# A two-layer hybrid trunk on one Trainium2 core: the residual kept token-major, with down and output projections that move 512 weight columns past stationary activations

## The chip, the cores and the metric

One core of a Trainium2 chip runs one program. The metric is the device time of one execution in microseconds (us), lower is better; each execution is one launch. Engines are named as the profile names them: PE is the matrix engine (PEld its weight loads), DVE, ACT and POOL work on elements, SP issues most transfers (SPq is its queue).

## The reference, cut to what matters

The input x is 256 tokens by 2048 features in fp32. Two layers follow, each with a mixer and a feed-forward part, all added to the residual x:

```python
for layer in range(2):
    h = rmsnorm(x, norm_w[layer, 0])
    x = x + (even_mixer(h, ...) if layer == 0 else odd_mixer(h, ...))
    h = rmsnorm(x, norm_w[layer, 1])
    x = x + swiglu(h, ffn_w_gu[layer], ffn_w_down[layer])
return rmsnorm(x, final_norm_w)
```

`even_mixer` is a projection, a causal convolution with layer norm, sparse attention and an output projection of 2048 by 2048. `odd_mixer` is a projection to 8192 columns, a gated recurrence in chunks and an output projection of 2048 by 2048. `swiglu` projects to two times 5632 columns and down to 2048. Five norms run over the 2048 features: two per layer and the final one.

## The kernel before, in words

**Layout.** Features lie on the partitions: the residual is 16 tiles `x[f]` of 128 features by 256 tokens. The normed activations lie so too, in 16 tiles `xhl(k)` (input of a stage) or `mhl(k)` (input of a down or output projection), each in two parts: a high part rounded to the engine's fp32r type and the low part that is left. A norm puts only its weight into the tile; the factor per token is applied when a product leaves PSUM (`self.bc`, one row of factors on all partitions).

**Weights.** `units` (lines 187 to 213) loads 1 MB of weights at a time into one of three `raw` buffers (SP queue), and ACT writes the high part `whi` and DVE (in part POOL) the low part `wlo`, 1024 columns of a partition at a time; three buffers of each. Each product is hi times hi, hi times lo and lo times hi.

**Two kinds of product.** `w_job` (215 to 247) makes 256 output features: each 128 by 128 block of weights is stationary and the activations of 256 tokens move past it. Its usual form has two matmuls for a block: the high weights past both parts of the activations (512 columns, line 240) and the low weights past the high part (256 columns, line 241; lines 237 and 238 for the last block), so a PSUM tile holds two halves that must be added. Its joint form has three matmuls of 256 columns (lines 233 to 235) and one sum. `x_job` (249 to 267) makes 512 output features for 128 tokens at a time: the activations are stationary, 512 weight columns move, three matmuls (lines 260 to 262) for each block of 128 features and each half `tb` of the tokens. Before the change only the odd mixer's `i` and `g` columns and the even mixer's values use it.

**Where the change lies.** The down projections of both layers (in `ffn`, three slabs of 16, 14 and 14 blocks of the hidden features, each with 8 chunks of 256 columns) and the odd output projection are `w_job`; the very last chunk of a layer and the even output projection are its joint form. Each finished tile `f` goes through `add_residual` (ACT copy, line 309, DVE add, 310, POOL add, 311; in the joint form one DVE add, 306) and, in the last slab or the mixer's last pass, `norm_tile`: ACT squares it, POOL adds the squares up (323), and `split` writes the parts of the next stage's `xhl` (ACT 139, DVE 140). `norm_done` calls `inv_rms`: matmuls with ones sum the squares over the partitions (160), DVE takes the root (146 to 151), and a matmul with a diagonal makes `self.bc` (177, 181). The final norm multiplies x by `bc` (1306) and stores it in four transfers.

**Order.** A scheduler orders instructions by a simulated timeline and by priorities (the work on finished tiles is raised by 600); each engine then runs its own list strictly in that order. Between `in_order()` and `traced = None` PE's order is instead the program's: the attention part of the even mixer with its first two output passes (input blocks 0 to 7 and 8 to 11), and the odd mixer up to the end of the first chunk of its output projection. The third even pass (blocks 12 to 15) and all of `ffn` are free. `drive` puts a list of background steps between the units of a list of jobs.

Of the kernel before, what the change touches and what calls it, by code (L numbers as in the profile page):

```python
# [10 lines left out]
F32 = mybir.dt.float32  # L11
# [21 lines left out]
COLS_B = (  # L33
    ("fnw", 16),
    ("convb", 8),
# [33 lines left out]
class Net:  # L69
# [82 lines left out]

    def inv_rms(self, sums, n, copy=True):


        nc = self.nc
        ps = self.mx()
        for tb in range(2):
            for i, q in enumerate(sums):
                nc.tensor.matmul(  # L160
                    ps[:, tb : tb + 1],
                    q[:, tb * 128 : tb * 128 + 128],
                    self.ones[:, 0:1],
                    start=(i == 0),
                    stop=(i == len(sums) - 1),
                )
        v = self.tile(self.tp, [128, 2], "rs_v", bufs=2)
        nc.vector.tensor_scalar(v, ps[:, 0:2], 1.0 / n, EPS, op0=ALU.mult, op1=ALU.add)
        tok = self.tile(self.tp, [128, 2], "rs_tok", bufs=2)
        self.rsqrt(tok, v, "rs")  # L170
        diag = self.t256("rs_diag", bufs=1)
        for tb in range(2):
            nc.vector.tensor_scalar(
                diag[:, tb * 128 : tb * 128 + 128], self.ca("ident"), tok[:, tb : tb + 1], None, op0=ALU.mult
            )
        pb = self.mx()
        nc.tensor.matmul(pb[:, :S], self.ones, diag, start=True, stop=True)
        if not copy:
            return tok, pb[:, :S]
        bc = self.t256("rs_bc", bufs=2)  # L180
        nc.scalar.copy(bc, pb[:, :S])
        return tok, bc
# [65 lines left out]

    def x_job(self, w, nkt, ncols, src, evac):

        nc = self.nc
        ps = [self.tile(self.ps_acc, [128, 512], "acc") for _ in range(2)]
        for k0, nu, hi, lo in self.units(w, nkt, ncols):
            last = k0 + nu == nkt
            for tb in range(2):
                t = slice(tb * 128, tb * 128 + 128)
                for i in range(nu):
                    k = k0 + i
                    o = ps[tb][:, :ncols]
                    nc.tensor.matmul(o, src(k)[:, 0, t], hi[:, i, :], start=(k == 0), stop=False)  # L260
                    nc.tensor.matmul(o, src(k)[:, 0, t], lo[:, i, :], start=False, stop=False)  # L261
                    nc.tensor.matmul(o, src(k)[:, 1, t], hi[:, i, :], start=False, stop=(k == nkt - 1))  # L262
                if last:
                    with self.tc.high_priority(offset=600):
                        evac(tb, ps[tb])
            yield

# [33 lines left out]

    def add_residual(self, f, ps, joint=False):
        nc = self.nc
        x = self.x[f]
        if joint:
            nc.vector.tensor_add(x, ps[:, :S], x)
            return
        c = self.t256("e_c")
        nc.scalar.copy(c, ps[:, S:])
        nc.vector.tensor_add(x, ps[:, :S], x)  # L310
        nc.gpsimd.tensor_add(x, x, c)  # L311

    def norm_tile(self, f, w, xhl):

        nc = self.nc
        x = self.x[f]
        if f == 0:
            self.ssq = self.t256("n_ssq", bufs=2)
            nc.scalar.activation(self.ssq, x, AF.Square)
        else:  # L320
            sq = self.t256("n_sq", bufs=2)
            nc.scalar.activation(sq, x, AF.Square)
            nc.gpsimd.tensor_add(self.ssq, self.ssq, sq)
        if xhl is not None:
            self.split(xhl(f), x, w[:, f : f + 1])

# [15 lines left out]
    def norm_done(self):  # L342
        self.tok, self.bc = self.inv_rms([self.ssq], D)

# [4 lines left out]

    def ffn(self, wgu, wdn, xhl, final_tile):  # L350
        nc = self.nc
        chunk = 0
        for s, (h0, nh) in enumerate(SLABS):
# [25 lines left out]
            jobs = []  # L379
            for c in range(8):  # L380

                def evac_d(nt, ps, c=c):
                    f = 2 * c + nt
                    self.add_residual(f, ps, joint=last and c == 7)
                    if last:
                        final_tile(f)

                jobs.append((-(-nh // 4), self.w_job(wdn[s][c], nh, mhl, evac_d, joint=last and c == 7)))
            self.drive(jobs)
# [3 lines left out]
    def even(self, xhl, start):  # L393
# [60 lines left out]
        def ln_steps():  # L454
# [24 lines left out]
            def root():  # L479
                self.rsqrt(st["r"], st["v"], "n_s")  # L480

# [65 lines left out]
        def evac_c(kv):  # L547
# [31 lines left out]
            [job(14 + i, evac_q(1, i)) for i in range(2)] + [job(10, evac_c(0)), job(11, evac_c(1))],  # L579
            ln_rest + [turn_gates, self.lower_bound],  # L580
            until=0.8,
# [16 lines left out]
        def evac_res(c, xhl2=None):  # L598
            def f(nt, ps):
                self.add_residual(2 * c + nt, ps, joint=True)  # L600
                if xhl2 is not None:
                    self.norm_tile(2 * c + nt, self.nw(1), xhl2)

            return f

        def out_jobs(k0, k1, xhl2=None):
            n = (k1 - k0 + 3) // 4 * 2
            src = lambda k: self.mhl(k0 + k)
            return [
                (n, self.w_job(wo[c, :, k0:k1], k1 - k0, src, evac_res(c, xhl2), joint=True)) for c in range(8)  # L610
            ]
# [372 lines left out]
    def odd(self, xhl):  # L984
# [245 lines left out]
        xhl2 = self.new_xhl()  # L1230

        def evac_res(c):
            def f(nt, ps):
                self.add_residual(2 * c + nt, ps)
                self.norm_tile(2 * c + nt, self.nw(3), xhl2)

            return f

        wo = a["od_out"]
        js = [(4, self.w_job(wo[c], KD, mhl, evac_res(c))) for c in range(8)]  # L1240
        self.drive(js[:1], O[3][1], until=0.75)
        self.traced = None
# [6 lines left out]
    def run(self):  # L1249
        nc, a = self.nc, self.a  # L1250
        self.cst_a = self.tile(self.fix, [128, NA], "cst_a")
        self.cst_b = self.tile(self.fix, [128, NB], "cst_b")
        nc.sync.dma_start(self.cst_a, a["cst_a"])
        xq = [self.tile(self.fix, [128, 4, S], f"x{i}") for i in range(4)]
        self.x = [xq[f // 4][:, f % 4, :] for f in range(KD)]
        self.ones = self.tile(self.fix, [128, 128], "ones")
        nc.vector.memset(self.ones, 1.0)
        self.mean1024 = self.tile(self.fix, [128, 128], "mean1024")
        nc.vector.memset(self.mean1024, 1.0 / 1024)

        xhl = self.new_xhl()
        sq = []

        def first_norm(i):

            x = xq[i]
            nc.sync.dma_start(x, a["x"][:, i * 4 : i * 4 + 4, :])
            w = self.nw(0)[:, i * 4 : i * 4 + 4].unsqueeze(2).to_broadcast([128, 4, S])
            xw = self.quarter(f"mhl{i}", (128, 2, 4, S), F32)
            nc.vector.tensor_mul(xw[:, 0], x, w)  # L1270
            xhl(4 * i)
            q = xhl.have[i]
            nc.scalar.activation(q[:, :, 0, :], xw[:, 0], AF.Copy)
            nc.vector.tensor_sub(q[:, :, 1, :], xw[:, 0], q[:, :, 0, :].bitcast(F32))  # L1274
            sq.append(xw[:, 1])
            with self.tc.high_priority(offset=-60):
                nc.scalar.activation(sq[i], x, AF.Square)
                if i:
                    nc.gpsimd.tensor_add(sq[0], sq[0], sq[i])

        def first_sums():
            first_norm(3)
            t = sq[0]
            nc.gpsimd.tensor_add(t[:, 0:2], t[:, 0:2], t[:, 2:4])
            nc.gpsimd.tensor_add(t[:, 0], t[:, 0], t[:, 1])
            self.ssq = t[:, 0]
            self.norm_done()

        first_norm(0)
        xhl = self.even(xhl, [lambda: first_norm(1), lambda: first_norm(2), first_sums])  # L1290

        nxt = self.new_xhl()
        self.ffn(a["gu0"], a["dn0"], xhl, lambda f: self.norm_tile(f, self.nw(2), nxt))
        xhl = self.odd(nxt)

        def last(f):
            self.norm_tile(f, None, None)
            x = self.x[f]
            nc.scalar.activation(x, x, AF.Copy, scale=self.cb("fnw")[:, f : f + 1])

        self.ffn(a["gu1"], a["dn1"], xhl, last)
        self.norm_done()
        bc = self.bc.unsqueeze(1)
        for i in (3, 0, 1, 2):
            eng = nc.gpsimd if i == 3 else nc.vector
            eng.tensor_mul(xq[i], xq[i], bc.to_broadcast([128, 4, S]))
            nc.sync.dma_start(a["out"][:, 4 * i : 4 * i + 4, :], xq[i])

# [108 lines left out]
```

## Time and profile before

| | |
|---|---|
| median of 3 runs | 2411.53 us (2409.87 to 2411.82) |
| the profiled execution's own time | 2411.09 us |
| its span in the trace | 2409.3 us |
| PE, share of the span | 98% |
| DVE, ACT, POOL | 64%, 49%, 26% |
| mean busy share of the 16 DMA engines | about 54% |

In the trace times run from the span's start. A row of a group gives line, engine, operation, output and inputs with shapes, count, busy time and the mean length of one. Matmuls are pipelined: the length of one is longer than the distance to the next, so PE's pace is read from starts and from whole stretches, not from lengths.

### The profile page before, as it was taken

How to read it: one execution, taken by the hardware profiler on the slowest of the kernel's cores; microseconds unless marked ns; L12 is line 12 of the kernel's file. 1: busy time of each engine (PE TensorE's matmuls, PEld its weight loads, DVE VectorE, ACT ScalarE, POOL GpSimd, SP SyncE). 2: the span in 40 equal slices, each digit the busy share in tenths (PEclk: the TensorE clock that was granted, in tenths of full speed). 3: DMA queues.
4: the chain of work that ended last, by engine and by line, in shares of the span. 5: the costliest groups of instructions: out<-in, count | busy, mean ns of one | idle time of the engine just before them, and what ended most of it. 6: DMA issues, size and time to landing. Idle time of an engine off the chain costs nothing.

```text
span 2409.3 us, 36579 instructions
## 1 busy us (share of the span) xinstructions
PE 2364.6 (98%) x14492; PEld 2086.6 (87%) x14492; DVE 1540.8 (64%) x2335; ACT 1173.1 (49%) x1729; POOL 625.2 (26%) x608
## 2 busy tenths in 40 slices
PE   6999999999999999999999999999999999999997
PEld 6999889888888888888888888888888888888886
DVE  7996578565555555657657777766555555555555
ACT  4435456554444544545544444455544445445454
POOL 5754524111111121114213333332111111121123
PEclk9999999999999999999999999999999999999998
DMA  6554524555555556555555445455555555565553
GB/s 208 176 174 154 179 78 151 193 188 183 189 192 189 180 183 200 188 180 186 195 178 175 159 156 175 140 185 185 190 192 183 186 191 192 175 194 191 192 175 123
DMA packets 62269, 427.88 MB, mean 178 GB/s; under 512 B 6928, under 2 KB 7056, under 8 KB 15248
## 3 DMA queue, kind: packets, MB, share of 16 engines
q1 hardware_dynamic: 61776, 425.01, 53.7%
q8 instruction: 113, 1.85, 0.3%
q10 hardware_dynamic: 320, 0.52, 0.1%
q14 instruction: 60, 0.49, 0.1%
HBM read 422.89 MB, written 2.10 MB: 176 GB/s over the span
## 4 chain that ended last, share of the span: by engine, by line
PE 94%; DVE 3%; issue 1%; POOL 1%; ACT 0%; DMA 0%; DVEq 0%; SPq 0%; POOLq 0%; ACTq 0%
PE acc L240 44%; PE acc L241 23%; PE acc L233 4%; PE acc L235 3%; PE acc L234 3%; PE acc L238 3%; PE acc L260 3%; PE acc L262 3%; PE acc L261 3%; PE acc L237 2%; PE mx L1089 1%; DVE wlo L208 1%; PE mx L677 1%; PE mx L855 0%; PE mx L782 0%
## 5 line engine op out<-in xcount | busy, mean ns | idle before, releaser
L208 DVE TENSOR_TENSOR wlo<-raw,whi 128x1024 fp32r<-128x1024 f32 (+1 forms) x749 | 959.0, 1281 | 659.7 <-ACT whi L207 648.3
L207 ACT ACTIVATE whi<-raw 128x1024 fp32r<-128x1024 f32 (+1 forms) x809 | 843.5, 1043 | 889.5 <-PE acc L240 596.7
L240 PE MATMUL acc<-xhl,whi 128*128 128x512 f32 x3120 | 1089.5, 395 | 0.0
L241 PE MATMUL acc<-xhl,wlo 128*128 128x256 f32 x3120 | 843.8, 280 | 0.0
L240 PEld LDWEIGHTS acc<-xhl,whi 128*128 128x128 f32 x3120 | 573.0, 188 | 113.0 <-issue 0.8
L241 PEld LDWEIGHTS acc<-xhl,wlo 128*128 128x128 f32 x3120 | 589.0, 189 | 25.1
L240 PE MATMUL acc<-mhl,whi 128*128 128x512 f32 x1500 | 520.1, 395 | 0.0
L241 PE MATMUL acc<-mhl,wlo 128*128 128x256 f32 x1500 | 398.7, 280 | 0.0
L297 POOL TENSOR_TENSOR e_u<-e_s,rs_bc 128x256 f32<-128x256 f32 x192 | 149.8, 781 | 937.7 <-DVE e_s L290 901.0
L240 PEld LDWEIGHTS acc<-mhl,whi 128*128 128x128 f32 x1500 | 273.9, 188 | 50.9
L241 PEld LDWEIGHTS acc<-mhl,wlo 128*128 128x128 f32 x1500 | 283.3, 189 | 15.4
L311 POOL TENSOR_TENSOR x<-x,e_c 128x256 f32<-128x256 f32 x108 | 109.1, 1023 | 422.0 <-DVE x L310 422.0
L208 POOL TENSOR_TENSOR wlo<-raw,whi 128x1024 fp32r<-128x1024 f32 (+1 forms) x60 | 145.2, 2421 | 141.3 <-ACT whi L207 130.4
L233 PE MATMUL acc<-xhl,whi 128*128 128x256 f32 (+1 forms) x528 | 149.8, 289 | 9.5 <-ACT whi L207 9.5
L235 PE MATMUL acc<-xhl,wlo 128*128 128x256 f32 (+1 forms) x528 | 150.2, 290 | 6.3 <-DVE wlo L208 4.0
L288 ACT COPY e_c<-acc 128x256 f32<-128x256 f32 x208 | 77.6, 373 | 157.9 <-PE acc L238 157.9
L234 PE MATMUL acc<-xhl,whi 128*128 128x256 f32 (+1 forms) x528 | 150.4, 288 | 1.4 <-DVE xhl L1274 1.4
L290 DVE TENSOR_TENSOR e_s<-acc,e_c 128x256 f32<-128x256 f32 x208 | 87.4, 422 | 67.6 <-ACT e_c L288 65.3
L261 PE MATMUL acc<-wlo,xhl 128*128 128x512 f32 x288 | 112.5, 391 | 0.0
L262 PE MATMUL acc<-whi,xhl 128*128 128x512 f32 x288 | 112.2, 390 | 0.0
L233 PEld LDWEIGHTS acc<-xhl,whi 128*128 128x128 f32 (+1 forms) x528 | 102.5, 195 | 9.7 <-ACT whi L207 9.5
L260 PE MATMUL acc<-whi,xhl 128*128 128x512 f32 x288 | 110.3, 395 | 0.0
(228 smaller groups left out, 2518.9 us busy)
## 6 DMA issues: line engine op xcount, KB each, us to landing
raw<-in_gu SPq DMA_DIRECT2D x176, 1024.0 KB, 5.0
raw<-in_dn SPq DMA_DIRECT2D x64, 1024.0 KB, 5.1
raw<-in_od_fq SPq DMA_DIRECT2D x32, 1024.0 KB, 5.0
raw<-in_od_ig SPq DMA_DIRECT2D x32, 1024.0 KB, 4.9
raw<-in_ev_in SPq DMA_DIRECT2D x30, 1024.0 KB, 5.0
raw<-in_dn SPq DMA_DIRECT2D x32, 768.0 KB, 4.4
raw<-in_od_out SPq DMA_DIRECT2D x16, 1024.0 KB, 5.0
raw<-in_ev_out SPq DMA_DIRECT2D x8, 1024.0 KB, 5.1
```

The source lines that it names most:

```text
L207: nc.scalar.activation(hi[:, :m], rs, AF.Copy)
L208: eng.tensor_sub(lo[:, :m], rs, hi[:, :m].bitcast(F32))
L233: nc.tensor.matmul(o[:, :S], h, a[:, 0, :], start=first, stop=False)
L234: nc.tensor.matmul(o[:, :S], h, a[:, 1, :], start=False, stop=False)
L235: nc.tensor.matmul(o[:, :S], l, a[:, 0, :], start=False, stop=end)
L240: nc.tensor.matmul(o, h, both, start=first, stop=False)
L241: nc.tensor.matmul(o[:, S:], l, a[:, 0, :], start=False, stop=False)
L260: nc.tensor.matmul(o, src(k)[:, 0, t], hi[:, i, :], start=(k == 0), stop=False)
L261: nc.tensor.matmul(o, src(k)[:, 0, t], lo[:, i, :], start=False, stop=False)
L262: nc.tensor.matmul(o, src(k)[:, 1, t], hi[:, i, :], start=False, stop=(k == nkt - 1))
L297: self.nc.gpsimd.tensor_mul(u, s, self.bc)
L311: nc.gpsimd.tensor_add(x, x, c)
```

## The change

The residual becomes one tile of tokens by features: partition t holds tokens t and 128 + t with all 2048 features. Down and output projections use `x_job` with 512 columns, four chunks in place of eight; `add_residual` is one DVE add of 128 by 512 from PSUM. For the three norms that feed a stage, `square` takes the sum of squares per token on ACT, and `turn_norm` turns each chunk's 8 blocks of 128 by 128 on PE into PSUM, from where `split` reads them. The sums lie per token, so the ones matmuls of these norms go. The first norm still reads a feature-major x, into scratch; the token-major copy is a second 2 MB load inside the even mixer. The final norm's weight is a 1 MB tile, spread over the partitions; x is stored in eight transfers.

```diff
-    def inv_rms(self, sums, n, copy=True):
+    def inv_rms(self, sums, n):
...
-        for tb in range(2):
-            for i, q in enumerate(sums):
-                nc.tensor.matmul(
-                    ps[:, tb : tb + 1],
-                    q[:, tb * 128 : tb * 128 + 128],
-                    self.ones[:, 0:1],
...
-        nc.vector.tensor_scalar(v, ps[:, 0:2], 1.0 / n, EPS, op0=ALU.mult, op1=ALU.add)
+        nc.vector.tensor_scalar(v, sums, 1.0 / n, EPS, op0=ALU.mult, op1=ALU.add)
...
-    def x_job(self, w, nkt, ncols, src, evac):
+    def x_job(self, w, nkt, ncols, src, evac, fine=False):
...
+                if fine and tb == 0:
+                    yield
...
+    def add_residual(self, c, tb, ps):
+        x = self.x[:, tb, c * 512 : c * 512 + 512]
+        self.nc.vector.tensor_add(x, ps, x)
+
+    def square(self, c, tb):
+        if c == 0 and tb == 0:
+            self.ss = self.tile(self.tp, [128, 2, 4], "n_ss", bufs=2)
+        sq = self.tile(self.tp, [128, 512], "n_sq", bufs=1)
+        self.nc.scalar.activation(
+            sq, self.x[:, tb, c * 512 : c * 512 + 512], AF.Square, accum_out=self.ss[:, tb, c : c + 1]
+        )
+
+    def turn_norm(self, c, w, xhl):
...
+        for f2 in range(4 * c, 4 * c + 4, 2):
+            pt = self.mx()
+            for i in range(4):
+                f, tb = f2 + i // 2, i % 2
+                x = self.x[:, tb, f * 128 : f * 128 + 128]
+                nc.tensor.transpose(pt[:, i * 128 : i * 128 + 128], x, self.ca("ident"))
+            for i in range(2):
+                f = f2 + i
+                self.split(xhl(f), pt[:, i * 256 : i * 256 + 256], w[:, f : f + 1])
+
+    def to_norm(self, w, xhl):
+        def f(c, tb):
+            self.square(c, tb)
+            if tb == 1:
+                self.turn_norm(c, w, xhl)
+        return f
...
     def norm_done(self):
-        self.tok, self.bc = self.inv_rms([self.ssq], D)
+        s = self.tile(self.tp, [128, 2], "n_s", bufs=2)
+        self.nc.vector.tensor_reduce(out=s, in_=self.ss, op=ALU.add, axis=AX.X)
+        self.tok, self.bc = self.inv_rms(s, D)
...
-                jobs.append((-(-nh // 4), self.w_job(wdn[s][c], nh, mhl, evac_d, joint=last and c == 7)))
+                jobs.append((nh // 2, self.x_job(wdn[s][c], nh, 512, mhl, evac_d)))
...
-            ln_rest + [turn_gates, self.lower_bound],
+            [lambda: nc.sync.dma_start(self.x, a["xt"])] + ln_rest + [turn_gates, self.lower_bound],
...
-                (n, self.w_job(wo[c, :, k0:k1], k1 - k0, src, evac_res(c, xhl2), joint=True)) for c in range(8)
+                (k1 - k0, self.x_job(wo[c, :, k0:k1], k1 - k0, 512, src, evac_res(c, xhl2), fine=True))
+                for c in range(4)
...
-        js = [(4, self.w_job(wo[c], KD, mhl, evac_res(c))) for c in range(8)]
-        self.drive(js[:1], O[3][1], until=0.75)
+        js = [(8, self.x_job(wo[c], KD, 512, mhl, evac_res(c))) for c in range(4)]
+        self.drive(js[:1], O[3][1], until=0.5)
...
+        def last(c, tb):
+            self.square(c, tb)
+            x = self.x[:, tb, c * 512 : c * 512 + 512]
+            eng = nc.vector if c == 3 else nc.gpsimd
+            eng.tensor_mul(x, x, fnw[:, c * 512 : c * 512 + 512])
+
+        nc.sync.dma_start(fnw, a["fnw"])
         self.ffn(a["gu1"], a["dn1"], xhl, last)
...
+        for c in range(4):
+            for tb in range(2):
+                x, r = self.x[:, tb, c * 512 : c * 512 + 512], tok[:, tb : tb + 1]
+                if (2 * c + tb) % 3 == 1:
+                    nc.scalar.activation(x, x, AF.Copy, scale=r)
+                else:
+                    nc.vector.tensor_scalar(x, x, r, None, op0=ALU.mult)
+                nc.sync.dma_start(a["out"][:, tb, c * 512 : c * 512 + 512], x)
```

The weights of these projections are laid out on the host in chunks of 512 columns in place of 256.

## Rows read from the trace of the kernel before

**Rows 1.** The page: busy time by engine, PE's granted clock in 40 slices, the chain.

```profile
PE 2364.6 (98%) x14492; PEld 2086.6 (87%) x14492; DVE 1540.8 (64%) x2335; ACT 1173.1 (49%) x1729; POOL 625.2 (26%) x608
...
PEclk9999999999999999999999999999999999999998
...
PE 94%; DVE 3%; issue 1%; POOL 1%; ACT 0%; DMA 0%; DVEq 0%; SPq 0%; POOLq 0%; ACTq 0%
```

**Rows 2.** Stretches: length, then busy us (instructions) by engine, granted clock, DMA share, GB/s.

```profile
594.79:684.39 89.60, 89.60 (x514) 78.40 (x513) 47.93 (x52) 39.74 (x50) 11.92 (x17) 1.00 0.58 188
841.19:919.86 78.67, 78.67 (x449) 68.65 (x448) 43.90 (x51) 35.47 (x50) 18.52 (x16) 1.00 0.58 191
1076.71:1155.62 78.91, 78.91 (x478) 70.11 (x477) 58.24 (x66) 46.04 (x78) 31.20 (x29) 1.00 0.58 191
1201.36:1244.90 43.54, 43.54 (x194) 36.04 (x192) 22.82 (x21) 19.97 (x21) 4.78 (x4) 1.00 0.58 194
1560.33:1651.00 90.67, 90.67 (x524) 79.34 (x523) 62.61 (x81) 49.66 (x79) 29.18 (x29) 1.00 0.54 177
2313.08:2391.99 78.91, 78.91 (x477) 70.09 (x475) 42.83 (x50) 44.91 (x76) 30.63 (x29) 1.00 0.46 150
248.85:395.00 146.15, 139.73 (x1176) 125.13 (x1175) 98.98 (x331) 76.15 (x199) 51.80 (x62) 0.98 0.36 119
395.00:414.02 19.02, 19.02 (x161) 19.02 (x160) 18.84 (x30) 16.31 (x33) 12.62 (x12) 1.00 0.70 232
```

**Rows 3.** PE's timeline in the third even output pass: start, length, line, instruction.

```profile
413.54 0.28 PE L235 MATMUL acc<-mhl,wlo 128*128 128x256 f32 x1
...
413.90 0.28 PE L235 MATMUL acc<-mhl,wlo 128*128 128x256 f32 x1
```

**Rows 4.** The chain in the odd mixer, at one of its transposes (start, us on the chain).

```profile
1345.24 0.87 PE mx L1212 x8
```

**Rows 5.** The group of these transposes: count, then busy us and mean ns of one.

```profile
L1212 PE MATMUL mx<-cst_a,K 128*128 128x128 f32 x32 | 4.3, 272 | 0.0
```

**Rows 6.** The timeline after the even mixer's last tile (in brackets: idle before, releaser).

```profile
420.66 0.61 PE L160 MATMUL mx<-ones,n_ssq 128*128 128x1 f32 x4 [0.45 <-POOL n_ssq L323]
420.81 1.21 DVE L208 TENSOR_TENSOR wlo<-raw,whi 128x1024 fp32r<-128x1024 f32 x1
```

**Rows 7.** Groups of DVE, ACT and POOL on tiles like those of the change.

```profile
L1186 DVE COPY K<-mx 128x512 f32<-128x512 f32 x8 | 5.5, 687 | 4.4 <-PE mx L1180 4.4
...
L140 DVE SCALAR_TENSOR_TENSOR mhl<-mx,cst_b,mhl 128x256 fp32r<-128x256 f32 x16 | 7.0, 478 | 0.4 <-ACT mhl L139 0.2
...
L1188 ACT ACTIVATE o_sq<-mx 128x512 f32<-128x512 f32 x8 | 4.8, 597 | 7.3 <-DVE K L1186 7.3
...
L311 POOL TENSOR_TENSOR x<-x,e_c 128x256 f32<-128x256 f32 x108 | 109.1, 1023 | 422.0 <-DVE x L310 422.0
```

**Rows 8.** Transfers: count, KB each, median us from issue to landing.

```profile
raw<-in_ev_out SPq DMA_DIRECT2D x8, 1024.0 KB, 5.1
raw<-in_ev_out SPq DMA_DIRECT2D x16, 512.0 KB, 3.6
...
out<-x SPq DMA_DIRECT2D x4, 512.0 KB, 3.3
```

**Rows 9.** The timeline of the end, from PE's last projection matmul on.

```profile
2391.87 0.28 PE L235 MATMUL acc<-mhl,wlo 128*128 128x256 f32 x1
...
2392.18 0.42 DVE L306 TENSOR_TENSOR x<-acc,x 128x256 f32<-128x256 f32 x1 [0.29 <-PE acc L235]
...
2394.81 0.16 DVE L168 TENSOR_SCALAR rs_v<-mx 128x2 f32<-128x2 f32 x1 [2.20 <-PE mx L160]
...
2396.97 0.48 DVE L173 TENSOR_SCALAR rs_diag<-cst_a,rs_tok 128x128 f32<-128x128 f32 x2
...
2399.17 5.64 DVE L1306 TENSOR_TENSOR x<-x,rs_bc 128x1024 f32<-128x1024 f32 x3 [1.72 <-ACT rs_bc L181]
...
2400.42 4.75 SPq L1307 DMA_DIRECT2D out<-x  x4
```

More of the change, by code (lines that the diff above doesn't have):

```diff
@@ L33 @@
 COLS_B = (
-    ("fnw", 16),
     ("convb", 8),
@@ L151, in rsqrt @@
             nc.vector.scalar_tensor_tensor(y, q, 1.5, y, op0=ALU.add, op1=ALU.mult)
-    def inv_rms(self, sums, n, copy=True):
+    def inv_rms(self, sums, n):
         nc = self.nc
-        ps = self.mx()
-        for tb in range(2):
-            for i, q in enumerate(sums):
-                nc.tensor.matmul(
-                    ps[:, tb : tb + 1],
-                    q[:, tb * 128 : tb * 128 + 128],
-                    self.ones[:, 0:1],
-                    start=(i == 0),
-                    stop=(i == len(sums) - 1),
-                )
         v = self.tile(self.tp, [128, 2], "rs_v", bufs=2)
-        nc.vector.tensor_scalar(v, ps[:, 0:2], 1.0 / n, EPS, op0=ALU.mult, op1=ALU.add)
+        nc.vector.tensor_scalar(v, sums, 1.0 / n, EPS, op0=ALU.mult, op1=ALU.add)
         tok = self.tile(self.tp, [128, 2], "rs_tok", bufs=2)
@@ L177, in inv_rms @@
         nc.tensor.matmul(pb[:, :S], self.ones, diag, start=True, stop=True)
-        if not copy:
-            return tok, pb[:, :S]
         bc = self.t256("rs_bc", bufs=2)
@@ L298, in scaled @@
         return u
-    def add_residual(self, f, ps, joint=False):
-        nc = self.nc
[L304 to L325, printed above, removed]
+    def add_residual(self, c, tb, ps):
[9 more added lines that the diff above has]
+    def turn_norm(self, c, w, xhl):
+        nc = self.nc
+        for f2 in range(4 * c, 4 * c + 4, 2):
[13 more added lines that the diff above has]
+        return f
     def quarters(self, tag):
@@ L342, in norm_done, with ffn @@
     def norm_done(self):
-        self.tok, self.bc = self.inv_rms([self.ssq], D)
+        s = self.tile(self.tp, [128, 2], "n_s", bufs=2)
+        self.nc.vector.tensor_reduce(out=s, in_=self.ss, op=ALU.add, axis=AX.X)
+        self.tok, self.bc = self.inv_rms(s, D)
     def nw(self, i):
         return self.ca("nw")[:, i * 16 : i * 16 + 16]
-    def ffn(self, wgu, wdn, xhl, final_tile):
+    def ffn(self, wgu, wdn, xhl, final):
         nc = self.nc
@@ L379, in ffn, with evac_d @@
             jobs = []
[L380 to L384, printed above, removed]
+            for c in range(4):
+                def evac_d(tb, ps, c=c):
+                    self.add_residual(c, tb, ps)
                     if last:
-                        final_tile(f)
-                jobs.append((-(-nh // 4), self.w_job(wdn[s][c], nh, mhl, evac_d, joint=last and c == 7)))
+                        final(c, tb)
+                jobs.append((nh // 2, self.x_job(wdn[s][c], nh, 512, mhl, evac_d)))
             self.drive(jobs)
@@ L479, in root @@
             def root():
-                self.rsqrt(st["r"], st["v"], "n_s")
+                self.rsqrt(st["r"], st["v"], "ln")
             def out(h):
@@ L598, in evac_res, with f @@
         def evac_res(c, xhl2=None):
-            def f(nt, ps):
-                self.add_residual(2 * c + nt, ps, joint=True)
+            then = self.to_norm(self.nw(1), xhl2)
+            def f(tb, ps):
+                self.add_residual(c, tb, ps)
                 if xhl2 is not None:
-                    self.norm_tile(2 * c + nt, self.nw(1), xhl2)
+                    then(c, tb)
             return f
         def out_jobs(k0, k1, xhl2=None):
-            n = (k1 - k0 + 3) // 4 * 2
             src = lambda k: self.mhl(k0 + k)
             return [
-                (n, self.w_job(wo[c, :, k0:k1], k1 - k0, src, evac_res(c, xhl2), joint=True)) for c in range(8)
+                (k1 - k0, self.x_job(wo[c, :, k0:k1], k1 - k0, 512, src, evac_res(c, xhl2), fine=True))
+                for c in range(4)
             ]
@@ L1230, in odd, with f @@
         xhl2 = self.new_xhl()
+        then = self.to_norm(self.nw(3), xhl2)
         def evac_res(c):
-            def f(nt, ps):
-                self.add_residual(2 * c + nt, ps)
-                self.norm_tile(2 * c + nt, self.nw(3), xhl2)
+            def f(tb, ps):
+                self.add_residual(c, tb, ps)
+                then(c, tb)
             return f
         wo = a["od_out"]
-        js = [(4, self.w_job(wo[c], KD, mhl, evac_res(c))) for c in range(8)]
-        self.drive(js[:1], O[3][1], until=0.75)
+        js = [(8, self.x_job(wo[c], KD, 512, mhl, evac_res(c))) for c in range(4)]
+        self.drive(js[:1], O[3][1], until=0.5)
         self.traced = None
@@ L1253, in run @@
         nc.sync.dma_start(self.cst_a, a["cst_a"])
-        xq = [self.tile(self.fix, [128, 4, S], f"x{i}") for i in range(4)]
-        self.x = [xq[f // 4][:, f % 4, :] for f in range(KD)]
+        self.x = self.tile(self.fix, [128, 2, D], "x")
         self.ones = self.tile(self.fix, [128, 128], "ones")
@@ L1264, in first_norm @@
         def first_norm(i):
-            x = xq[i]
+            xw = self.quarter(f"mhl{i}", (128, 2, 4, S), F32)
+            x = xw[:, 1]
             nc.sync.dma_start(x, a["x"][:, i * 4 : i * 4 + 4, :])
             w = self.nw(0)[:, i * 4 : i * 4 + 4].unsqueeze(2).to_broadcast([128, 4, S])
-            xw = self.quarter(f"mhl{i}", (128, 2, 4, S), F32)
             nc.vector.tensor_mul(xw[:, 0], x, w)
@@ L1274, in first_norm @@
             nc.vector.tensor_sub(q[:, :, 1, :], xw[:, 0], q[:, :, 0, :].bitcast(F32))
-            sq.append(xw[:, 1])
+            sq.append(x)
             with self.tc.high_priority(offset=-60):
-                nc.scalar.activation(sq[i], x, AF.Square)
+                nc.scalar.activation(x, x, AF.Square)
                 if i:
@@ L1285, in first_sums @@
             nc.gpsimd.tensor_add(t[:, 0], t[:, 0], t[:, 1])
-            self.ssq = t[:, 0]
-            self.norm_done()
+            ps = self.mx()
+            for tb in range(2):
+                nc.tensor.matmul(
+                    ps[:, tb : tb + 1], t[:, 0, tb * 128 : tb * 128 + 128], self.ones[:, 0:1], start=True, stop=True
+                )
+            self.tok, self.bc = self.inv_rms(ps[:, 0:2], D)
         first_norm(0)
@@ L1292, in run @@
         nxt = self.new_xhl()
-        self.ffn(a["gu0"], a["dn0"], xhl, lambda f: self.norm_tile(f, self.nw(2), nxt))
+        self.ffn(a["gu0"], a["dn0"], xhl, self.to_norm(self.nw(2), nxt))
         xhl = self.odd(nxt)
[L1296 to L1299, printed above, removed]
-        self.ffn(a["gu1"], a["dn1"], xhl, last)
[L1302 to L1307, printed above, removed]
+        fw = self.ctx.enter_context(self.tc.tile_pool(name="fw", bufs=1))
+        fnw = self.tile(fw, [128, D], "fnw")
+        def last(c, tb):
[4 more added lines that the diff above has]
+        nc.sync.dma_start(fnw, a["fnw"])
+        self.ffn(a["gu1"], a["dn1"], xhl, last)
+        s = self.tile(self.tp, [128, 2], "n_s", bufs=2)
+        nc.vector.tensor_reduce(out=s, in_=self.ss, op=ALU.add, axis=AX.X)
+        nc.vector.tensor_scalar(s, s, 1.0 / D, EPS, op0=ALU.mult, op1=ALU.add)
+        tok = self.tile(self.tp, [128, 2], "rs_tok", bufs=2)
+        self.rsqrt(tok, s, "rs")
+        for c in range(4):
+            for tb in range(2):
+                x, r = self.x[:, tb, c * 512 : c * 512 + 512], tok[:, tb : tb + 1]
[4 more added lines that the diff above has]
+                nc.sync.dma_start(a["out"][:, tb, c * 512 : c * 512 + 512], x)
 def _chunks(w, ncols):
@@ L1357 @@
     arr = {"x": np.ascontiguousarray(i["x"][0].T.reshape(KD, 128, S).transpose(1, 0, 2))}
+    arr["xt"] = np.ascontiguousarray(i["x"][0].reshape(2, 128, D).transpose(1, 0, 2))
+    arr["fnw"] = np.ascontiguousarray(np.broadcast_to(i["final_norm_w"][None], (128, D)))
     w = i["ev_w_in"][0]
@@ L1373 @@
     wo = np.concatenate([wo[:1024], wo[1024:].reshape(16, 64, D)[order].reshape(1024, D)], 0)
-    arr["ev_out"] = _chunks(wo, 256)
+    arr["ev_out"] = _chunks(wo, 512)
     w1 = i["ev_cmp_w1"][0]
@@ L1380 @@
     arr["od_ig"] = _chunks(w[:, 4096:8192], 512)
-    arr["od_out"] = _chunks(i["od_w_out"][0], 256)
+    arr["od_out"] = _chunks(i["od_w_out"][0], 512)
     for l in range(2):
@@ L1385 @@
         for s, (h0, nh) in enumerate(SLABS):
-            arr[f"dn{l}_{s}"] = _chunks(i["ffn_w_down"][l][h0 * 128 : (h0 + nh) * 128], 256)
+            arr[f"dn{l}_{s}"] = _chunks(i["ffn_w_down"][l][h0 * 128 : (h0 + nh) * 128], 512)
     c = dict(con)
     c["nw"] = _cols(i["norm_w"])
-    c["fnw"] = _cols(i["final_norm_w"])
     c["convb"], c["lnw"], c["lnb"] = (_cols(i[n]) for n in ("ev_conv_b", "ev_conv_ln_w", "ev_conv_ln_b"))
@@ L1409 @@
         a[f"dn{l}"] = [a[f"dn{l}_{s}"] for s in range(len(SLABS))]
-    a["out"] = nc.dram_tensor("out", [128, KD, S], F32, kind="ExternalOutput").ap()
+    a["out"] = nc.dram_tensor("out", [128, 2, D], F32, kind="ExternalOutput").ap()
     with tile.TileContext(nc, schedule_with_timeline_sim=True) as tc:
@@ L1415 @@
     out = np.asarray(r.results[0]["out"])
-    return np.ascontiguousarray(out.transpose(2, 1, 0).reshape(1, S, D))
+    return np.ascontiguousarray(out.transpose(1, 0, 2).reshape(1, S, D))
```

## The prediction

> **What bounds the kernel now.** The page comes first: PE is busy for 98% of the span, its granted clock is at the upper of its two levels (2.4 GHz) in all but the last slice, and the chain that ended last is PE for 94% [rows 1]. So only two things change the time: what PE needs for its columns, and what PE waits for. The other engines (DVE 64%, ACT 49%, POOL 26%) matter only where PE waits for them. Second, the stretches of the projections [rows 2]: in the first slab of a down projection (594.79 to 684.39 us) PE is busy without a break, and so in the others; DVE needs 48 of its 90 us. Only the attention part (248.85 to 395.00) holds idle PE time, 146.15 - 139.73 = 6.4 us. Third, the pace. Both forms stream the same number of columns (768 for a block of 128 by 128 weights and 256 tokens), so a gain must come from fewer instructions for them, and this is read from whole stretches.
>
> **PE's pace, form by form.** Usual `w_job`: the first slab has 16 blocks by 16 tiles, 256 pairs in 89.60 us, 350 ns a pair. Joint form: three matmuls start within 413.90 - 413.54 = 0.36 us [rows 3], 360 ns. `x_job`: from 1201.36 to 1244.90 PE does nothing but the odd mixer's first `i` and `g` jobs, 2 times 96 matmuls of 512 columns in 43.54 us [rows 2], 226.8 ns each; 768 columns are 1.5 of them, 340.2 ns.
>
> **The sum, part by part.**
>
> Feed-forward down projections: a layer takes 89.60 + 78.67 + 78.91 = 247.2 us, and the second layer repeats this within 0.1 us [rows 2]: 494.4. After: 44 blocks by 4 chunks by 6 matmuls by 0.2268 = 239.5 a layer, 479.0. **Minus 15.4.**
>
> Odd output projection: 90.67 us [rows 2], of which 0.87 are transposes of the recurrence [rows 4], 89.8. After: 16 by 4 by 6 by 0.2268 = 87.1. **Minus 2.7.**
>
> Even output projection: 256 joint triples at 0.36 = 92.2, after 87.1. **Minus 5.1.**
>
> Turning for three norms: 16 tiles by 2 by 3 = 96 transposes. Eight such fp32 transposes take 0.87 us of the chain [rows 4], 0.109 each: **plus 10.4**, all on PE's path. They have no cover.
>
> Ones matmuls of the same norms: 3 by 0.61, and 0.45 idle before one of them [rows 6]: **minus 2.3**. The DVE reduction that replaces them is off PE, and `self.bc` is first wanted when the next stage's first job ends, 16 by 2 pairs = 11 us later.
>
> Elementwise work: an ACT copy, a DVE add and POOL's add of 1.02 us a tile become one DVE add of about 0.69 us a chunk half (the copy of 128 by 512 from PSUM) [rows 7]. This lies beside PE: **zero**. The tightest place is the third even pass, where DVE is busy for 18.84 of 19.02 us [rows 2]. There a new chunk costs DVE 2 by 1.21 for `wlo` [rows 6], 2 by 0.69, and 4 by 0.478 for the splits [rows 7]: 5.7 us, against 24 by 0.2268 + 0.87 = 6.3 on PE. DVE is still covered, by 0.6 us; without that cover each chunk would cost the difference.
>
> The added wait: a chunk's transposes stand in PE's list behind the DVE add of its last half, and every matmul of the next chunk listed after them waits too. The odd projection's first chunk is in program order, so nothing stands between: 0.1 to start, half a `wlo` ahead on DVE (0.6), the add 0.69, about 1.4 us. The other 11 are placed by the scheduler's timeline, with matmuls of the next chunk ahead of them. The nearest row is the ones matmul, placed in the same way: 0.45 us idle in one norm of three [rows 6], so 0.15 on average. I take 0.3 each, between these two: 1.4 + 3.3, **plus 4.7**. Ends: 0, and 12 times a whole `wlo`, the start and the add, 2.0 each, 24.
>
> The end: from the last matmul's start (2391.87) the old tail takes 17.4 us [rows 9]. New, from the same point: the add starts at 0.42 (0.31 in the row, and 0.11 for the longer matmul), takes 0.69, the square 0.6 and 0.2 for its sum, the product with the weight 0.69: 2.6. One reduction (0.2) and the root as before (2396.97 - 2394.81 = 2.2): 5.0. A first scaling, 0.7: 5.7. Then 2 MB go out: 3.3 us for the first 512 KB and 1.5 for each further (5.1 - 3.6) [rows 8], 7.8, and 0.8 as after the old last landing (2400.42 + 4.75 + 3.3 against 2409.3): 14.3. **Minus 3.0.** POOL's sums, a matmul and ACT's copy are gone, but the stores become what is late. Ends: 0 (eight smaller stores cost more) and minus 6 (the stores overlap the scaling wholly).
>
> New loads: the 2 MB x waits in SP's queue ahead of weights for up to 4 by 1.5 = 6.0 us [rows 8]. A `raw` buffer feeds PE 16 by 0.36 = 5.8 us, and one more is loaded ahead: **zero**, at most 6. The norm weight's 1 MB costs half of that at most; zero.
>
> The attention part, where PE's list is rebuilt around other units: **zero**, ends minus 6.4 (all idle time goes) and plus 6.4 (it doubles).
>
> Sum: -15.4 - 2.7 - 5.1 + 10.4 - 2.3 + 4.7 - 3.0 = -13.4. The profiled execution took 2411.09 us, so 2397.7; the median of the runs shown lies 0.4 above it. Forecast: **2398 us**.
>
> **The rivals.**
>
> *PE waits at the turns.* If DVE always has a `wlo` of 1.21 us in hand when a chunk ends, each of the 12 turns costs up to 2.0 us in place of 0.4: +19.3, 2417 us, slower. It decides from a mean wait of (15.4 + 2.7 + 5.1 - 10.4 + 2.3 + 3.0) / 12 = 1.5 us a chunk on; below that the change still gains. For it: PE is strictly in order, and ready-as-early-as-possible placing leaves no slack. Against it: the transposes of the recurrence never let PE idle [rows 5], DVE is idle for nearly half of the down stages, and the raised priority brings the add ahead. Waits of 0.9 to 2.0 us (2405 to 2417): 0.15.
>
> *The columns set the pace, not the instructions.* If 512 moving columns past activations run no faster per column than the pairs, the 18.1 us of the down and odd projections vanish: 2416 us. Against it stands the one clean stretch, 192 matmuls in 43.54 us [rows 2]; that was with `xhl` of 2048 features, and the new jobs read `mhl` in the same layout. The Trainium skill's page "TensorE: Matmul & The Clock Gate" (section "Back-to-back issue gap") speaks for it: it gives a gap of N/2.4 + 2.5 ns, by which a pair would take 325.0 and 1.5 long matmuls 323.7, an estimate of 2 us for all that. The trace disagrees with that figure: 350 and 340. Chance 0.05.
>
> *Turned blocks cost their full length.* The mean length of a transpose is 272 ns [rows 5]; if PE does not overlap them, 96 cost 26.1 in place of 10.4, and the time is 2414 us. Against it: eight in 0.87 us [rows 4]. The same page's section "PE-mode transpose" names about 275 ns in a kernel's context; the row's length agrees, its distance does not. Chance 0.04.
>
> *More than forecast.* No waits (-4.7), the best end (-3.0 more), part of the attention's idle time (up to 6.4): 2384 to 2392. Chance 0.12.
>
> **How the numbers follow.** The forecast's own range is 2392 to 2405, chance 0.64. A difference of about 0.2% (4.8 us) is what a measurement of this kernel can tell from no change, so faster means below 2406.7 and slower above 2416.3. Faster: 0.64, 0.12, and 0.03 of the waits: 0.79. Same: 0.08 of the waits, 0.03 and 0.03 of the next two rivals: 0.14. Slower: 0.04, 0.02 and 0.01: 0.07. The range 2388 to 2410 leaves out the best cases below (about 0.06) and the heavy waits and the two price rivals above (about 0.14).
>
> **What would show it.** Matmuls of line 260 to 262 on `mhl` 226.8 ns apart in the down stages, a slab of 14 blocks in 76.2 us and one of 16 in 87.1: right. 96 transposes 0.109 apart, and PE idle before them by some tenths of a us, with the odd projection's first chunk the worst, released by DVE's add. POOL nearly empty in the output and down stages. From the last matmul to the end about 14 us, with the transfers last. Wrong would be a DVE add or `wlo` that PE waits for over 1.5 us a chunk, a spacing near 350 / 1.5 = 233, or PE waiting for weights around the second load of x.

## The result, and the profile after

The changed kernel takes 2395.09 us (median of 5 runs, 2393.35 to 2395.38), the kernel before 2410.88 beside it (5 runs, 2409.87 to 2411.82): 15.8 us less, a ratio of 0.9934 with a 95% interval of 0.9921 to 0.9948. The forecast was 2398, range 2388 to 2410. The profiled execution took 2393.35, its span 2391.6; the span before was 2409.3.

The page of the changed kernel: busy time by engine, the granted clock, the chain. Against [rows 1] PE has 1194 instructions fewer and is as busy in share as before; POOL lost a quarter of its work (625 to 458 us); its share of the chain stays at 1%.

```profile
PE 2348.2 (98%) x13298; PEld 2024.4 (85%) x13298; DVE 1492.0 (62%) x2245; ACT 1129.8 (47%) x1591; POOL 458.1 (19%) x445
...
PEclk8999999999999999999999999999999999999999
...
PE 96%; DVE 2%; POOL 1%; issue 0%; ACT 0%; DMA 0%; DVEq 0%; SPq 0%; POOLq 0%; ACTq 0%
```

The stretches that answer to [rows 2]: length, then busy us (instructions) of PE, PEld, DVE, ACT, POOL, granted clock, DMA share, GB/s.

```profile
592.80:679.86 87.06, 87.06 (x385) 72.10 (x384) 45.09 (x44) 34.88 (x35) 1.60 (x2) 1.00 0.57 193
836.70:912.88 76.18, 76.18 (x337) 63.06 (x336) 40.19 (x40) 30.64 (x31) 1.60 (x2) 1.00 0.57 193
1069.72:1148.65 78.93, 78.93 (x361) 65.50 (x360) 45.18 (x52) 39.19 (x55) 1.60 (x2) 1.00 0.55 187
1553.87:1644.71 90.84, 90.84 (x420) 75.39 (x418) 53.81 (x71) 43.64 (x60) 2.94 (x2) 1.00 0.55 188
2302.07:2378.26 76.19, 76.19 (x337) 62.88 (x335) 40.50 (x38) 32.74 (x42) 10.49 (x8) 1.00 0.45 152
249.72:395.00 145.28, 139.33 (x887) 107.98 (x886) 99.49 (x317) 78.33 (x202) 50.94 (x62) 0.99 0.38 130
395.00:412.26 17.26, 17.26 (x89) 14.36 (x88) 13.25 (x20) 11.82 (x26) 0.00 (x0) 1.00 0.52 175
```

A slab of 16 blocks takes 87.06 us in place of 89.60, one of 14 takes 76.18 in place of 78.67: the forecast said 87.1 and 76.2. The slab that feeds a norm (1069.72) and the odd output projection (1553.87) hardly changed, 78.93 against 78.91 and 90.84 against 90.67: what the pace gives there, the transposes take back (24 of each stage's 32 lie in its stretch, the last 8 in the stage after it). PE has no idle time in any of these projections. In the third even pass, from 395.00 on, DVE, which was busy for 18.84 of 19.02 us, now has 13.25 of 17.26.

What PE does around a turn, here of the third slab's first chunk in layer 0 (PE's timeline: start, length, line, instruction):

```profile
1088.78 0.62 PE L247 MATMUL acc<-whi,mhl 128*128 128x512 f32 x2
...
1093.31 0.40 PE L249 MATMUL acc<-whi,mhl 128*128 128x512 f32 x1
1093.55 0.38 PE L313 MATMUL mx<-cst_a,x 128*128 128x128 f32 x2
1093.69 0.48 PE L247 MATMUL acc<-whi,mhl 128*128 128x512 f32 x1
1094.01 0.81 PE L313 MATMUL mx<-cst_a,x 128*128 128x128 f32 x6
1094.58 0.48 PE L248 MATMUL acc<-wlo,mhl 128*128 128x512 f32 x1
```

and DVE's two adds of this chunk (DVE's timeline of the same kernel):

```profile
1088.50 1.28 DVE L294 TENSOR_TENSOR x<-acc,x 128x512 f32<-128x512 f32 x2
```

The adds end at 1089.8, the transposes (line 313) start at 1093.55. The scheduler put sixteen matmuls of the next chunk ahead of them (12 to 16 at the 12 turns), so nothing waits. Of all waits of PE in this kernel, none is at line 313; its group says so by its last number, the idle time before it:

```profile
L313 PE MATMUL mx<-cst_a,x 128*128 128x128 f32 x96 | 14.3, 272 | 0.0
```

The end, from PE's last matmul on (timeline; in brackets the idle time before, and the releaser), against [rows 9]:

```profile
2378.03 0.39 PE L249 MATMUL acc<-whi,mhl 128*128 128x512 f32 x1
...
2378.45 0.69 DVE L294 TENSOR_TENSOR x<-acc,x 128x512 f32<-128x512 f32 x1 [0.44 <-PE acc L249]
...
2379.24 0.63 ACT L301 ACTIVATE n_sq<-x 128x512 f32<-128x512 f32 x1 [0.47 <-DVE x L294]
...
2379.99 0.69 DVE L1312 TENSOR_TENSOR x<-x,fnw 128x512 f32<-128x512 f32 x1 [0.25 <-ACT n_sq L301]
...
2383.03 2.07 DVE L1327 TENSOR_SCALAR x<-x,rs_tok 128x512 f32<-128x512 f32 x5
2383.54 4.47 SPq L1328 DMA_DIRECT2D out<-x  x8
```

From 2378.03 to the span's end at 2391.57 are 13.5 us; before the change they were 17.4. The first scaling starts 5.0 us after the last matmul, as forecast, and what comes last are the stores.

### The profile page after: what moved, and what is told of

The parts are those of the page before. It is cut to its first block, busy times and chain, and to the rows that moved or that the text cites. A ratio compares the mean times of both kernels' runs of the same rounds, so it can differ in the third digit from the quotient of the medians.

```text
span 2391.6 us, 33510 instructions
## 1 busy us (share of the span) xinstructions
PE 2348.2 (98%) x13298; PEld 2024.4 (85%) x13298; DVE 1492.0 (62%) x2245; ACT 1129.8 (47%) x1591; POOL 458.1 (19%) x445
## 4 chain that ended last, share of the span: by engine, by line
PE 96%; DVE 2%; POOL 1%; issue 0%; ACT 0%; DMA 0%; DVEq 0%; SPq 0%; POOLq 0%; ACTq 0%
PE acc L227 30%; PE acc L228 15%; PE acc L247 12%; PE acc L249 12%; PE acc L248 12%; PE acc L222 2%; PE acc L220 2%; PE acc L221 2%; PE acc L225 2%; PE acc L224 1%; PE mx L1093 1%; PE mx L681 1%; PE mx L313 0%; DVE wlo L195 0%; DVE a_z L829 0%
## 5 line engine op out<-in xcount | busy, mean ns | idle before, releaser
L195 DVE TENSOR_TENSOR wlo<-raw,whi 128x1024 fp32r<-128x1024 f32 x733 | 935.2, 1276 | 710.3 <-ACT whi L194 703.6
L194 ACT ACTIVATE whi<-raw 128x1024 fp32r<-128x1024 f32 x793 | 840.2, 1060 | 967.8 <-PE acc L249 420.5
L248 PE MATMUL acc<-wlo,mhl 128*128 128x512 f32 x960 | 375.0, 391 | 0.0
L249 PE MATMUL acc<-whi,mhl 128*128 128x512 f32 x960 | 374.7, 390 | 0.0
L247 PE MATMUL acc<-whi,mhl 128*128 128x512 f32 x960 | 349.2, 395 | 0.0
L247 PEld LDWEIGHTS acc<-whi,mhl 128*128 128x128 f32 x960 | 180.4, 188 | 40.8 <-issue 4.0
L249 PEld LDWEIGHTS acc<-whi,mhl 128*128 128x128 f32 x960 | 180.6, 188 | 37.7
L248 PEld LDWEIGHTS acc<-wlo,mhl 128*128 128x128 f32 x960 | 180.7, 188 | 35.8
L279 DVE TENSOR_TENSOR e_s<-acc,e_c 128x256 f32<-128x256 f32 x208 | 87.1, 420 | 70.5 <-ACT e_c L277 70.5
L249 PE MATMUL acc<-whi,xhl 128*128 128x512 f32 x288 | 112.3, 390 | 0.0
L220 PEld LDWEIGHTS acc<-xhl,whi 128*128 128x128 f32 (+1 forms) x528 | 102.0, 193 | 10.4 <-ACT whi L194 10.2
```

The lines of the kernel that those rows point to most:

```text
L194: nc.scalar.activation(hi[:, :m], rs, AF.Copy)
L195: eng.tensor_sub(lo[:, :m], rs, hi[:, :m].bitcast(F32))
L220: nc.tensor.matmul(o[:, :S], h, a[:, 0, :], start=first, stop=False)
L279: nc.vector.tensor_add(s, ps[:, :S], c)
```

## The experiments

Seven runs, each timed beside the kernel before, which took 2410.97 to 2411.34 us beside them; line numbers of their rows are their own.

**The control.** The changed kernel again, to compare the others with.

> The changed kernel unaltered, as the control for the three runs beside it. All theories: 2395 us within 2, some 16 us below the kernel before.

Measured: 2394.97 us, ratio 0.9935 (0.9920 to 0.9949).

**Turns twice.** What do the transposes cost?

```diff
-            for i in range(4):
+            for i in (0, 1, 2, 3, 0, 1, 2, 3):
                 f, tb = f2 + i // 2, i % 2
```

> Each of the 96 transposes is issued twice into the same place; nothing else changes. Theory (the turns lie on PE's path at 0.109 us each): 96 by 0.109 = 10.4 us more than the control, 2405.5. Rival (PE has slack around them, so they are covered): within 2 us of the control.

Measured: 2405.23 us, 10.3 more than the control (ratio to before 0.9977, 0.9968 to 0.9986). The stages of the control and then of this kernel (stretches, columns as above):

```profile
1071.05:1149.98 78.93, 78.93 (x361) 65.48 (x360) 45.19 (x52) 39.19 (x55) 1.60 (x2) 1.00 0.55 187
1555.15:1646.00 90.85, 90.85 (x420) 75.39 (x418) 53.83 (x71) 43.64 (x60) 2.95 (x2) 1.00 0.54 187
```

```profile
1074.56:1156.13 81.57, 81.57 (x385) 68.10 (x384) 45.47 (x52) 39.33 (x55) 1.60 (x2) 1.00 0.53 181
1562.20:1655.66 93.46, 93.46 (x443) 78.03 (x442) 54.05 (x71) 43.78 (x60) 2.95 (x2) 1.00 0.54 182
```

Each stretch holds 24 transposes more and is 2.6 us longer: 0.11 each, wholly on PE's path. The cover that the rival supposed does not exist.

**256 columns.** Is it the number of columns that move, or the lighter work on finished tiles? The weights of these projections are laid out in chunks of 256 again, and the residual stays token-major:

```diff
-            for c in range(4):
+            for c in range(8):
...
-                jobs.append((nh // 2, self.x_job(wdn[s][c], nh, 512, mhl, evac_d)))
+                jobs.append((-(-nh // 4), self.x_job(wdn[s][c], nh, 256, mhl, evac_d)))
```

(and so in the two output projections, `add_residual`, `square`, `turn_norm` and `last`).

> The same token-major residual, but the down and output projections move 256 weight columns at a time in place of 512 (twice the matmuls and weight loads for the same columns). Theory (the gain is PE's pace, a fixed cost for each instruction): 768 columns take 360 ns as the joint form of the kernel before in place of 340.2, and 1920 blocks of 768 columns make 38 us more than the control, 2433, slower than the kernel before. Rival (the gain is that ACT, DVE and POOL have less to do for a finished tile): the projections keep their time, within 4 us of the control.

Measured: 2429.1 us, 34.1 more than the control and slower than the kernel before (ratio 1.0077, 1.0062 to 1.0092). Its first down slab and the one that feeds a norm:

```profile
596.21:688.37 92.16, 92.16 (x770) 92.16 (x768) 46.96 (x52) 34.88 (x35) 1.59 (x2) 1.00 0.57 183
1082.72:1166.30 83.58, 83.58 (x701) 83.58 (x700) 48.38 (x66) 44.46 (x77) 1.59 (x2) 1.00 0.55 180
```

768 matmuls in 92.16 us are 120 ns each, just the joint form's pace [rows 3]; the slab has twice the instructions for the same columns and is 5.1 us longer than the 87.06 of 512 columns, as expected. POOL is as empty (1.59 us) and DVE hardly busier than in the changed kernel, so the relief of these engines is not where the gain comes from. Of the 4 us that are missing from the expected 38, 3.1 lie in the even output projection with the attention: it was expected to take 5.1 us longer and took 2.0 (163.15 to 165.11 us), with 4.1 us of idle PE time in place of 6.0. Another 1.2 us were saved at the end, from the last matmul on, where the last chunk is smaller.

**Turns in order.** PE's list is forced to the program's in the stages that feed a norm:

```diff
+            if last:
+                self.in_order()
             self.drive(jobs)
+            self.traced = None
```

(in `ffn`; in the mixers `self.traced = None` moves behind the output projection).

> The order of PE's list is forced to the program's in the three stages that feed a norm, so that the transposes of a chunk stand right behind its last matmul (9 of the 12 chunks; after a stage's last chunk the next stage stays free). Theory (the scheduler hides DVE's add of 0.68 us by listing later matmuls first): each of the 9 turns now waits for the add, 0.8 to 2.0 us, in all 7 to 18 us more than the control, 2402 to 2413. Rival (PE would not wait there in any order, the add being done in time): within 2 us of the control.

Measured: 2402.89 us, 7.9 more than the control (ratio to before 0.9968, 0.9957 to 0.9980). The same two stretches, and PE and DVE at one turn:

```profile
1074.46:1156.39 81.93, 80.24 (x361) 65.40 (x360) 45.47 (x52) 38.99 (x55) 1.60 (x2) 1.00 0.52 180
1561.64:1655.50 93.86, 92.11 (x420) 75.32 (x418) 54.07 (x71) 43.43 (x60) 2.94 (x2) 1.00 0.53 182
```

```profile
1093.84 0.68 DVE L294 TENSOR_TENSOR x<-acc,x 128x512 f32<-128x512 f32 x1
1093.97 0.14 PEld L313 LDWEIGHTS mx<-cst_a,x 128*128 128x128 f32 x1 [0.72 <-DVE x L294]
...
1094.57 0.75 PEld L313 LDWEIGHTS mx<-cst_a,x 128*128 128x128 f32 x7 [0.46 <-DVE x L294]
```

Three forced turns make each stretch 3.0 us longer than the control's, 1.0 us a turn, and the even output projection 3.2. The trace as a whole is 9.5 us longer, the medians differ by 7.9. So the wait that the forecast's rival named is a real price, and the order alone avoids it. At all nine forced turns PE is idle for 0.56 to 0.62 us and the first transpose starts 0.06 us after the first half's add, so DVE had no `wlo` in hand that would have doubled the price.

**The load of x held back.** The trace of the changed kernel showed what no step of the forecast has: the 2 MB load, written in the text at a background step of the even mixer, waits for nothing there, and the scheduler issued it among the first transfers (SP's queue, start and length of the issue):

```profile
5.29 0.47 SPq L566 DMA_DIRECT2D cst_b<-in_cst_b  x1
5.85 0.57 SPq L582 DMA_DIRECT2D x<-in_xt  x1
11.80 24.31 SPq L183 DMA_DIRECT2D raw<-in_ev_in  x5
```

The experiment gives it something to wait for:

```diff
+        def load_x():
+            nc.gpsimd.tensor_copy(self.x[:, :, 0:1], vt[1].rearrange("p (a b) -> p a b", a=2)[:, :, 0:1])
+            nc.sync.dma_start(self.x, a["xt"])
...
-            [lambda: nc.sync.dma_start(self.x, a["xt"])] + ln_rest + [turn_gates, self.lower_bound],
+            [load_x] + ln_rest + [turn_gates, self.lower_bound],
```

> The 2 MB load of the token-major x is held back until the even mixer's values exist (one column of x is first written from them), where the diff's text has it; in the changed kernel's trace the load is issued 5.8 us after the start, among the first loads. Theory (there it takes transfer time from the first weights): the first matmul of the even output projection comes 0.9 to 1.6 us earlier than the control's 250.4 us in the trace, and later weights still arrive in time, since one raw buffer feeds PE for 5.8 us and 2 MB take about 6: 2394 us. Rival (the late start is not the load's doing, and held back it makes PE wait for weights around 200 us): the output projection starts up to 6 us later, 2395 to 2401.

Measured: 2390.85 us (ratio 0.9916, 0.9902 to 0.9929), 4.1 below the control by medians. The two intervals of the ratio overlap a little, but the slowest of its five runs (2391.98) is faster than the fastest of the control's four (2393.87). The first matmul of the even output projection comes at 247.8 us, 2.6 before the control's; the profiled runs as a whole differ by 2.7 (spans 2390.2 and 2392.9), so the 1.4 more by the medians has no place in these traces. The first 45 us, of the kernel before, the changed one and this one in turn:

```profile
0.00:45.00 45.00, 26.12 (x158) 24.99 (x159) 33.98 (x41) 20.44 (x22) 22.36 (x16) 0.96 0.69 231
```

```profile
0.00:45.00 45.00, 23.94 (x148) 22.61 (x149) 31.64 (x41) 19.50 (x22) 21.52 (x17) 0.85 0.67 255
```

```profile
0.00:45.00 45.00, 28.00 (x185) 26.81 (x186) 37.27 (x39) 19.36 (x20) 25.94 (x17) 0.95 0.66 234
```

With the load among the first ones PE is busy for 23.94 us in place of 28.00 and its granted clock averages 0.85 between its two levels in place of 0.95; more bytes arrive (255 GB/s), but the weights come later. The first 512 KB behind the load, issued at 11.8 us, take 10.1 us from issue to landing in the changed kernel and 5.4 in this one:

```profile
raw<-in_ev_in SPq DMA_DIRECT2D x1, 512.0 KB, 10.1
```

```profile
raw<-in_ev_in SPq DMA_DIRECT2D x1, 512.0 KB, 5.4
```

In these 45 us PE waits 21.1 us in all in the changed kernel, 5.0 of them for `wlo` on DVE, and 17.0 in this one, 0.4 of them for `wlo` on DVE. Held back, the load is issued at 166 us; from 160 to 260 us PE waits 1.9 us in all, for two conversions on POOL and for no transfer, as in the control. The rival is out; the theory undersized the gain.

**Gate and up projections too.** If the pace by instructions is the reason, the largest projection should gain as well, at the price of turning its product:

```diff
-SLABS = ((0, 16), (16, 14), (30, 14))
+SLABS = ((0, 16), (16, 16), (32, 12))
...
+                def evac_a(tb, ps, G=G):
+                    G[tb] = self.tile(gh, [128, 512], "f_G", bufs=4)
+                    nc.scalar.activation(G[tb], ps, AF.Silu, scale=self.tok[:, tb : tb + 1])
...
+                    nc.vector.scalar_tensor_tensor(
+                        H[tb], ps, self.tok[:, tb : tb + 1], G[tb], op0=ALU.mult, op1=ALU.mult
+                    )
...
+                jobs.append((8, self.x_job(wgu[chunk], KD, 512, xhl, evac_a)))
+                jobs.append((8, self.x_job(wgu[chunk + 1], KD, 512, xhl, evac_b)))
```

> The gate and up projections of both feed-forward parts also move 512 weight columns past stationary activations; the product is scaled per token as it leaves PSUM, and its 44 blocks a layer are turned on PE (176 transposes more); slabs of 16, 16 and 12 blocks, as chunks are four blocks wide. Theory (pace by instructions, turns at their price, no waits): 2816 blocks of 768 columns at 340.2 in place of 350 ns are 27.6 us less, 176 by 0.1 to 0.109 are 17.6 to 19.2 more; 8 to 10 us below the control, 2385 to 2387, the fastest so far. Rival (PE waits for the elementwise work in front of the turns, about 1 us for each of the 22 chunks as in the forced order): the gain of 9 becomes a loss of up to 13, 2395 to 2408.

Measured: 2386.62 us (ratio 0.9899, 0.9885 to 0.9912), 8.4 below the control. Its first gate and up slab, and the next down slab:

```profile
413.67:591.96 178.29, 178.29 (x804) 147.66 (x803) 92.41 (x106) 81.33 (x97) 0.00 (x0) 1.00 0.55 189
...
591.96:679.93 87.97, 87.97 (x394) 72.85 (x392) 45.55 (x45) 35.10 (x36) 0.00 (x0) 1.00 0.56 191
```

PE has no idle time and POOL nothing to do; PE does not wait at the 22 turns.

**Both.**

> The gate and up projections token-major and the load of x held back, together. Theory (the two gains lie in different stages, the one in PE's pace, the other in the first 45 us, so they add): 2386.6 less 4.1 = 2382.5 us, within 1.5. Rival (the load, now among other work, or the changed list of the scheduler takes back one of them): 2386 or more.

Measured: 2382.12 us (2381.82 to 2383.87; ratio to before 0.9882, 0.9865 to 0.9898), against 2411.34 of the kernel before beside it. This is the fastest version, 13 us below the change; holding back the load is worth 4.5 us here and 4.1 without the other edit.

## Why the prediction was right

**The pace was the gain, and sized right.** The three projection terms (15.4, 2.7 and 5.1) rest on 226.8 ns for a matmul of 512 columns, read from the 43.54 us of the one clean stretch [rows 2]; the down slabs came out at 87.06 and 76.18 us where 87.1 and 76.2 were forecast. The run with 256 columns shows the cause: same layout, same engines relieved, twice the instructions, and the projections cost more than before. Between 256 and 512 columns a matmul with its weight load grows from 120 to 226.8 ns, 0.417 ns a column, and what is left of either is a fixed 13.2 ns. So the rival by which columns alone set the pace is out. The Trainium skill's page "TensorE: Matmul & The Clock Gate" (section "Back-to-back issue gap") gives N/2.4 + 2.5 ns for a matmul taken alone, an estimate of 109.2 and 215.8 ns for these two. No stretch here runs at it: they take 120 and 226.8.

Three things stay open. By these prices the usual pair should take 226.8 + 120 = 346.8 ns and took 350: of the 9.8 ns gained on a block, 6.6 come from fewer instructions, and for 3.2 no run shows the reason. And the fixed part does not hold below 256 columns: a transpose moves 128 and adds 0.109 us, and ten of the odd mixer's products of 128 columns take 1.11 us of the chain before the change, where 128 by 0.417 and 13.2 ns would give 0.067 each. PEld is busy throughout the slab of 256 columns (92.16 us of 92.16), and for 72.10 of 87.06 us with 512; whether the weight load or the matmul sets the 120 ns, no run separates.

**The turns cost what the chain said.** 10.4 us were set down for 96, doubling them costs 10.3. Their length in the group is 272 ns, but each adds about 0.11 us; the rival that took the length is out.

**The wait at the turns failed as a term.** The forecast took 4.7 us: 1.4 for the odd projection's first chunk, "in program order, so nothing stands between", and 0.3 for the other 11. All are zero. At the 12 turns the scheduler left 2.2 to 3.8 us between the add and the first transpose, so none of the 0.3 us each was paid. For the first chunk the reading of the code was wrong: the order is forced among instructions written before `traced = None`, and the matmuls of the next chunk are written after it, so they may pass the transposes, and did (16 matmuls, 3.7 us, lie between the second add of that chunk, done at 1577.7, and its turn at 1581.4). Forced into order a turn does cost 1.0 us, where 1.4 was set down for the one turn taken to be forced: the mechanism exists, and what was wrong is that this kernel would meet it.

**The end** was forecast to save 3.0 and saved 17.4 - 13.5 = 3.9.

**The loads were set to zero, and that was wrong**, in place and size. The cover named (a buffer ahead in the even mixer) does exist there, as the held-back load shows, but the load did not run there. Among the first transfers it has no cover: it holds the next weights back by 4.7 us (10.1 - 5.4; the forecast had allowed up to 6.0), and costs 1.9 to 2.6 us by the start of the even output projection in the traces (249.7 and 250.4 against 247.8) and 4.1 us by the medians. Against the kernel before only 0.9 to 1.6 us of it show, because with the load held back this projection starts 1.0 us earlier than in the kernel before (248.85), for a reason that no run isolates.

The traces allow the same sum by stage, each from its first matmul to the next stage's. Change in us against the kernel before; 24 of the 32 transposes of each norm stand in the stage that makes its input, 8 in the next:

| Stage | forecast | changed kernel | control |
|---|---|---|---|
| up to the even output projection | 0 | +0.9 | +1.6 |
| even output projection with the attention | -2.5 | -2.6 | -2.0 |
| six down slabs | -12.8 | -12.9 | -12.9 |
| odd output projection | -0.1 | +0.2 | +0.2 |
| gate and up projections, odd mixer | +0.3 | +0.6 | +0.6 |
| the end | -3.0 | -3.9 | -3.8 |
| waits at the turns | +4.7 | 0 | 0 |
| sum (of unrounded numbers) | -13.4 | -17.7 | -16.4 |

The two profiled runs lie 17.7 and 16.4 us below the kernel before's, the medians 15.8. So the stages were sized well; of the three misses, the waits took 4.7 us that never came, the end saved 0.9 more than forecast, and the start cost 0.9 to 1.6 that was set to zero. That the forecast of 2398 lies only 3 us above the measured 2395 owes something to this: without the waits it would have been 2393, below the result. What the attention part did by itself stays open: its idle time went from 6.4 to 5.9 us, and in the 256-column run a reshuffled list moved its stage by some 3 us.

## What to carry to other kernels

On a PE-bound kernel, compare two forms of a product by whole stretches per column: here a pair of weight load and matmul costs some 13 ns beyond its 256 or 512 columns, so moving 512 columns per load beats 256. It pays for turning the result on PE only where enough matmuls stand behind each turned block: 128 features of the output cost two transposes, 0.218 us, and gain 9.8 ns for each block of weights, so about 22 blocks are the break-even against the usual form. A layer's down projection has 44; the odd output projection has 16, and became no faster. A turn behind an elementwise add needs other matmuls listed between them; look in the trace for idle time before the transposes, not for their length. After moving a tensor, look up where its load was really issued: here a transfer that waits for nothing was issued at 5.85 us, though its text stands in the middle of the even mixer.

## What was not expected of the hardware

A 2 MB load among the first ones lowers PE's busy time in the first 45 us by 4 us, though the transfers move more bytes (255 against 234 GB/s): the weights behind it in the queue come later (10.1 us from issue to landing in place of 5.4), and the granted clock, 0.95 on average without it, is 0.85 with it. And the cost of a matmul with its weight load is not one fixed part and one part per column over all widths: 226.8 ns for 512 columns and 120 for 256, but still 109 to 111 for 128.
